# The low part of each split weight tile: an accumulating transfer in place of a GpSimd subtraction

## The chip, the core and the metric

The kernel runs on one core of a Trainium2 chip. The core has a matrix engine (TensorE, PE in the rows; its weight loads are PEld), VectorE (DVE), ScalarE (ACT), GpSimd (POOL), a queue engine that issues most transfers (SP), and 16 DMA engines that carry the transfers of all queues. The metric is the device time of one execution in microseconds, as a median over runs.

## The reference

Two layers of a diffusion backbone work on 128 context tokens and 512 latent tokens at once, with 1024 channels. Each layer has a mixing block and a SwiGLU FFN, and nearly all weight arithmetic is plain products of float32 arrays:

```python
proj = h @ p['w_in']
...
merged = (gates[:, :, 0] * (y_a @ p['w_pa']) + gates[:, :, 1] * (y_b @ p['w_pb'])
          + gates[:, :, 2] * (y_c @ p['w_pc']))
return merged.astype(h.dtype) @ p['w_o'], s_fin
...
gu = h @ w_gu
gate, up = jnp.split(gu, 2, axis=-1)
return (jax.nn.silu(gate) * up) @ w_down
```

Here `y_a` comes from a chunked gated DeltaNet, `y_b` from a long convolution and `y_c` from a Fourier mixer. Each sub-layer is preceded by an RMSNorm with shifts and scales that come from a conditioning vector through `w_mod`.

## The kernel before

**Split products.** Activations stand as channels on the 128 partitions by 640 tokens, which are worked on in two chunks of 320. TensorE multiplies in a rounded float32 form (`F32R`). So that the product is exact enough, each operand is cut into a high part, its rounding, and a low part, what the rounding left over; `mm3` then makes three matmuls for each 128 x 128 block of weights: high by high, high by low, low by high. `gemm` runs `mm3` over the blocks of a tile for one chunk of tokens.

**Weights.** Each weight is used once per execution. `wplan` lists raw tiles (128 x 1024, 512 KB, two buffers with the tag `wr`) in the order of use, and units of up to 512 columns that are split at once. `wload` issues raw loads on SP's queue. `wsplit` makes the two parts of a unit: ScalarE rounds it into `wh`, GpSimd subtracts the rounding from the raw values into `wl`. Each of the two tags has four buffers that turn; some units are parked in wide `A` tiles in their place. `free` is called when the last use of a unit has been issued, and splits further units up to four ahead of the one in use. `wget` and `wuse` hand the parts to the products.

**The FFN.** For all but two of a layer's 22 hidden tiles, gate and up are made by `pair`: seven products over blocks in place of eight. A pair has two raw tiles and seven units: three are quarters of the raw tiles, four are sums of quarters that VectorE makes in `U` tiles (`wsum`). Each product is 12 matmuls of 320 columns, in `prod`, which frees its unit at its end. After every three or four hidden tiles come eight output tiles of the down projection, whose units serve 18 or 24 matmuls.

**Order.** The instruction streams are written out by the program itself. A planner (`tick`) counts an estimated end for each instruction on five clocks (`pe`, `dve`, `act`, `pool`, `dma`). Side streams (the DeltaNet scans, filters, norms, and the conditioning columns that VectorE makes from `w_mod` loads) give steps that `pump` puts between the matmuls when their inputs are due by these clocks. Every engine runs its own stream in order, and waits on semaphores. The planner charges a GpSimd subtraction of 512 columns 0.1 + 512/450 us on `pool`; a `dma_start` from any engine is charged on `dma`, by bytes plus 2.0 us:

```python
if eng == "dma" or op == "dma_start":
    t = max(t, c["dma"], c["pe"] if cur is None else cur.t0) + n * out.shape[0] * 4 / 3.6e5
    c["dma"] = t
    t += 2.0
```

All instructions go through one helper, so nearly all rows name line 2185, and are told apart by tile names.

Of the kernel before, what the change touches and what calls it, by code (L numbers as in the profile page):

```python
# [71 lines left out]
def _plan():  # L72
    """the order of use: whole tiles, and pairs of a gate and an up tile for the seven products"""
    p = [("w", k) for k in _stream() if k[0] not in ("g", "u", "d")]
    for kind, g in _ffn_order():
        if kind == "gu":
            for j in GROUPS[g]:
                p += [("s", j)] if j >= WHOLE else [("w", ("g", j)), ("w", ("u", j))]
        else:
            p += [("w", ("d", g, m)) for m in range(0, 8, 2)]  # L80
    return p
# [9 lines left out]
def _parked(key):  # L91
    """whether the split tile stays for one half of the tokens after the other, in a place of its own"""
# [13 lines left out]
# ---------------------------------------------------------------- tables that depend on shapes alone  # L106
# [126 lines left out]
# ---------------------------------------------------------------- layout of the inputs  # L233
# [67 lines left out]
class _Net:  # L301
# [21 lines left out]
    # ---- allocation  # L323
# [19 lines left out]
    def xps(self):  # L343
        """a bank of either pool"""
        self.nps += 1
        return self.ps() if self.nps % 2 else self.gps()
# [8 lines left out]
    # ---- background work: each step of a side stream is issued once the tensor engine's work issued  # L355
    # so far reaches, by the engines' rates, the time when the step's inputs are there
    def when(self, *aps):
        """the time when what was issued has written these"""
# [36 lines left out]
    def on(self, *tiles):  # L395
        """the next step of the stream that runs needs these"""
        self.cur.t = max(self.cur.t, self.when(*[x[:] if not hasattr(x, "ap") else x for x in tiles]))

    def at(self, *tiles):
        """the next step of the stream that runs needs these and nothing of its other steps"""  # L400
# [7 lines left out]
    def ready(self, co):  # L408
        """a stream may yield a test (the time when it is met, or None) or a time its next step may
        be issued early"""  # L410
# [18 lines left out]
    def pump(self):  # L429
        """the streams' ready steps, as long as the main stream keeps its share of the tensor engine"""  # L430
# [19 lines left out]
    def finish_one(self, cos):  # L450
        """the next step of several streams, or of one that they wait for"""
# [6 lines left out]
    def stagger(self, gens, width):  # L458
        """several streams, `width` at a time, each behind the one before it"""
# [32 lines left out]
    # ---- weights  # L492
    def wplan(self, depth):
        """raw tiles in the order of their loads, and units: up to 512 columns that are split at once"""
# [24 lines left out]
    def wload(self, need=-1):  # L519
        """loads of raw tiles up to `need`, and further ones whose room is free by now"""  # L520
# [10 lines left out]
    def wsum(self, r, x):  # L531
        """sums of the four blocks of a gate and an up tile"""
# [12 lines left out]
    def wsplit(self, n):  # L545
        """units up to n, split in two float32r parts"""
        nc = self.nc
        while self.nunit <= n:
# [10 lines left out]
            else:  # L559
# [3 lines left out]
                lo = self.pw.tile([P, 512], F32R, tag="wl", name=self.nm("wl"), bufs=4)  # L563
            nc.scalar.copy(hi[:, :w], src)
            nc.gpsimd.tensor_tensor(out=lo[:, :w], in0=src, in1=hi[:, :w].bitcast(F32), op=ALU.subtract)
# [10 lines left out]
    def wget(self, key):  # L576
        """the units of the next item: all at once, or of a pair one after the other"""
# [13 lines left out]
    def lots(self, n):  # L591
        """places for the next n parked units"""
# [6 lines left out]
    def free(self, seen, drop):  # L599
        """so many more units have come to use, and so many of those in turning buffers had their last"""  # L600
# [32 lines left out]
    def rsqrt(self, r, m):  # L633
        """r = m ** -0.5, Newton's steps from a guess by the bits of m"""
# [9 lines left out]
    # ---- start  # L644
# [30 lines left out]
    def mods(self, l, lo, hi, par=False, ahead=1, hint=0.5):  # L675
        """adaLN columns lo..hi (of 48) of layer l, one per output channel tile"""
# [43 lines left out]
    def mods_pe(self):  # L720
        """the first 4 * MP adaLN columns of layer 0, on the tensor engine"""
# [45 lines left out]
    # ---- RMSNorm  # L767
    def sq_add(self, k, c=None):
        """running sum of the squares of x's channel tile k, on all tokens or a chunk of them"""
# [11 lines left out]
    def rstd(self, u, n, w):  # L781
        """1 / rms(x) of n * w tokens from u on, on all partitions"""
# [23 lines left out]
    def wait(self, c):  # L806
        """for 1 / rms(x) of a chunk"""
# [3 lines left out]
    def norm(self, l, gcol, sh, scl, new, place):  # L811
        """h = rmsnorm(x) * (1 + sc) + sh, split in two float32r parts"""
# [37 lines left out]
    def need(self, n):  # L850
        """steps of the norm until n channel tiles of chunks of h are issued"""
# [13 lines left out]
    def norm_blocks(self, l, gcol, sh, scl):  # L865
        """h by blocks (half of the channels) x (half of the tokens), and the sums of blocks for the seven
        products"""
# [34 lines left out]
    # ---- x in and out of DRAM  # L902
# [4 lines left out]
    # ---- Hyena's filters  # L907
    def sin_mlp(self, ps, M, scale, bias, out, n):
        """out = sin(scale * ps + bias), the argument brought within half a turn first"""
# [15 lines left out]
    def filters(self, l):  # L925
        """spectra of the two-sided filters of both orders, kept in DRAM"""
# [44 lines left out]
        def weights(z, o):  # L971
            """taps of h0 + h1 (real part) or h0 - h1 (imaginary part)"""
# [87 lines left out]
    # ---- input projection  # L1060
    def evict(self, dst, ps, c, func=AF.Copy, scale=1.0):
        """dst[:, 0:640] gets a chunk of 320 tokens"""
        self.nc.scalar.activation(dst[:, c * NC:(c + 1) * NC], ps[:, :NC], func, scale=scale)

    def conv_tile(self, wcol, l, raw=None, o=None):
        """room for a channel tile before and after the centred three-tap convolution: 128 prompt columns,
        one unused, 512 sample columns"""
# [21 lines left out]
    def proj_conv(self, key, wcol, l):  # L1089
        """one channel tile through w_in and the convolution"""  # L1090
# [6 lines left out]
    def permute(self, dst, src, fn, goff=1):  # L1097
        """token order of the delta tiles: tile s < 4 holds sample chunks s and 7 - s, tile 4 the prompt"""
# [6 lines left out]
    # ---- gated DeltaNet  # L1105
# [1130 lines left out]
```

## Time and profile before

| | us |
|---|---|
| median of 3 runs | 2922.06 |
| lowest and highest | 2921.55, 2927.12 |
| span of the profiled execution | 2920.5 |
| TensorE busy in it | 2570.7 (88%) |
| VectorE busy | 2191.0 (75%) |
| GpSimd busy | 1372.3 (47%) |
| ScalarE busy | 1017.4 (35%) |

The profiled execution has no time of its own besides its span, which is 1.6 us below the median of the runs. Matmuls overlap in the pipeline, and each is shown with its whole latency, so their pace is read from the starts of a group and not from the mean duration of one. A wait is named by what released it. Busy time of an engine leaves out the sequencer's work, the issuing of transfers among it.

### The profile page before, as it was taken

What the parts mean: (1) busy time and instruction counts of PE and PEld (TensorE: products, weight loads), DVE (VectorE), ACT (ScalarE), POOL (GpSimd) and SP (SyncE); (2) the same over time, 40 slices, a digit from 0 to 9 for tenths busy, and PEclk for the clock granted to TensorE, in tenths of its full rate; (3) what the DMA queues carried; (4) which work ended last, traced back from release to release, by engine and by line L of the source; (5) the groups of instructions that cost most, each with busy time, mean ns of one, the idle gap of its engine ahead of it and who ended that gap; (6) DMA issues with size and microseconds to landing.
All of it is one profiled execution on the core that took longest, in us unless ns stands there. A gap on an engine that the chain in (4) does not pass through costs nothing. (4 is left out here: it accounts for less than half of the span.)

```text
span 2920.5 us, 53508 instructions
## 1 busy us (share of the span) xinstructions
PE 2570.7 (88%) x20996; PEld 2423.8 (83%) x20996; DVE 2191.0 (75%) x4162; ACT 1017.4 (35%) x2148; POOL 1372.3 (47%) x1228
## 2 busy tenths in 40 slices
PE   5897879879998888888898988788899988999998
PEld 1686878879998888878897768788899988999997
DVE  7787996774647899889966679977746468877665
ACT  2454223322332243223334552333323322444342
POOL 2333425442335475555543436353523354777662
PEclk8898989989999899999998999899999998999999
DMA  7442221343554223333322221212335542222222
GB/s 277 143 151 84 71 83 54 103 144 130 201 185 152 86 90 114 105 118 105 109 96 93 94 88 68 83 53 97 134 130 199 187 152 73 66 80 88 79 80 80
DMA packets 112044, 330.35 MB, mean 113 GB/s; under 512 B 12186, under 2 KB 26522, under 8 KB 103776
## 3 DMA queue, kind: packets, MB, share of 16 engines
q1 hardware_dynamic: 110352, 319.06, 31.9%
q0 software_dynamic: 1440, 7.87, 0.8%
q8 instruction: 165, 2.70, 0.4%
q14 instruction: 87, 0.71, 0.1%
HBM read 294.89 MB, written 37.24 MB: 114 GB/s over the span
## 5 line engine op out<-in xcount | busy, mean ns | idle before, releaser
L2185 PE MATMUL pg<-A,wh 128*128 128x320 f32 (+1 forms) x6304 | 1491.7, 324 | 115.3 <-DVE T L2185 46.5
L2185 PEld LDWEIGHTS pg<-A,wh 128*128 128x128 f32 (+1 forms) x6304 | 1096.4, 196 | 168.7 <-issue 56.5
L2185 POOL TENSOR_TENSOR wl<-wr,wh 128x512 fp32r<-128x512 f32 (+2 forms) x486 | 694.5, 1444 | 813.0 <-ACT wh L2185 773.9
L2185 PE MATMUL pg<-A,wl 128*128 128x320 f32 (+1 forms) x3152 | 1005.9, 319 | 1.3 <-POOL wl L2185 1.1
L2185 PEld LDWEIGHTS pg<-A,wl 128*128 128x128 f32 (+1 forms) x3152 | 618.0, 196 | 4.6 <-POOL wl L2185 3.4
L2185 ACT CAST wh<-wr 128x512 fp32r<-128x512 f32 (+2 forms) x486 | 284.4, 611 | 399.6 <-PE pg L2185 287.6
L2185 PE MATMUL ps<-A,wh 128*128 128x320 f32 x1696 | 386.7, 315 | 15.4 <-ACT wh L2185 15.4
L2185 DVE CUSTOM_DVE_ANT_0 A<-U,A 128x512 f32<-128x512 f32 x336 | 324.8, 967 | 14.3 <-DMA U<-in_wmod_dram 7.0
L2185 PEld LDWEIGHTS ps<-A,wh 128*128 128x128 f32 x1696 | 292.1, 193 | 16.9 <-ACT wh L2185 16.7
L2185 PE MATMUL ps<-A,wl 128*128 128x320 f32 x848 | 268.4, 316 | 8.0 <-POOL wl L2185 7.7
L2185 PE MATMUL ps<-A,A 32*32 32x32 f32 (+5 forms) x2984 | 212.1, 248 | 51.1 <-DVE A L2185 49.3
L2185 POOL TENSOR_TENSOR wl<-U,wh 128x512 fp32r<-128x512 f32 x160 | 238.2, 1509 | 30.7 <-ACT wh L2185 30.6
L2185 PEld LDWEIGHTS ps<-A,A 32*32 32x32 f32 (+2 forms) x2984 | 183.7, 150 | 63.1 <-DVE A L2185 50.6
L2185 DVE TENSOR_TENSOR A<-A 128x120 f32<-128x120 f32 (+22 forms) x690 | 209.5, 367 | 11.7 <-DMA A<-hyS 8.8
L2185 POOL TENSOR_TENSOR A<-A,A 128x640 fp32r<-128x640 f32 (+5 forms) x84 | 121.0, 1453 | 161.0 <-ACT A L2185 153.0
L2185 PE MATMUL pg<-A,A 128*128 128x320 f32 x1056 | 168.2, 319 | 10.0 <-ACT A L2185 9.6
L2185 PEld LDWEIGHTS ps<-A,wl 128*128 128x128 f32 x848 | 163.6, 193 | 12.0 <-POOL wl L2185 11.9
L2185 PEld LDWEIGHTS pg<-A,A 128*128 128x128 f32 x1056 | 162.7, 195 | 12.7 <-ACT A L2185 9.8
L2185 DVE TENSOR_TENSOR T<-T,T 128x320 f32<-128x320 f32 (+1 forms) x139 | 120.8, 869 | 68.0 <-ACT T L2185 63.0
L2185 ACT CAST wh<-U 128x512 fp32r<-128x512 f32 x160 | 99.1, 621 | 168.5 <-PE pg L2185 51.3
L2185 DVE STREAM_TRANSPOSE A<-A 32x1024 f32<-32x1024 f32 x72 | 148.8, 2092 | 1.3
L2185 DVE TENSOR_TENSOR U<-ps,U 128x512 f32<-128x512 f32 x144 | 78.0, 543 | 92.0 <-PE ps L2185 64.8
(164 smaller groups left out, 3085.8 us busy)
## 6 DMA issues: line engine op xcount, KB each, us to landing
wr<-in_wbig_dram SPq DMA_DIRECT2D x272, 512.0 KB, 3.7
U<-in_wmod_dram SPq DMA_DIRECT2D x168, 256.0 KB, 4.3
A<-hT SPq DMA_DIRECT2D x32, 1024.0 KB, 8.7
kSp<-U SPq DMA_DIRECT2D x40, 256.0 KB, 2.0
U<-kSp SPq DMA_DIRECT2D x40, 256.0 KB, 5.5
hyS<-T SPq DMA_DIRECT2D x24, 320.5 KB, 3.3
A<-in_wm_dram SPq DMA_DIRECT2D x6, 1024.0 KB, 11.0
A<-in_cc_dram SPq DMA_DIRECT2D x6, 1024.0 KB, 5.3
```

What stands on the lines that cost most here:

```text
L2185: return f(*a, **k)
```

## The change

In `wsplit`, ScalarE writes the negated rounding of the unit into the low buffer (a copy with scale -1 into an `F32R` tile). A transfer on GpSimd's queue then adds the raw unit onto it, element by element, in the DMA engines. ScalarE's rounding copy into the high buffer comes after these two in program order. The GpSimd subtraction is gone.

```diff
                 hi = self.pw.tile([P, 512], F32R, tag="wh", name=self.nm("wh"), bufs=4)
                 lo = self.pw.tile([P, 512], F32R, tag="wl", name=self.nm("wl"), bufs=4)
+            nc.scalar.activation(lo[:, :w], src, AF.Copy, scale=-1.0)
+            nc.gpsimd.dma_start(lo[:, :w], src, accum_op=ALU.add)
             nc.scalar.copy(hi[:, :w], src)
-            nc.gpsimd.tensor_tensor(out=lo[:, :w], in0=src, in1=hi[:, :w].bitcast(F32), op=ALU.subtract)
             self.whl[self.nunit] = (hi, lo)
```

The rest of the diff takes out comments and docstrings. The splits of activations (`split`) still subtract on GpSimd or VectorE.

## Rows read from the trace of the kernel before

**Rows 1.** First part of the page: busy time of each engine.
```profile
PE 2570.7 (88%) x20996; PEld 2423.8 (83%) x20996; DVE 2191.0 (75%) x4162; ACT 1017.4 (35%) x2148; POOL 1372.3 (47%) x1228
```

**Rows 2.** Stretches of both FFNs: us; PE, PEld, DVE, ACT, POOL; clock; DMA; GB/s.
```profile
1035.00:1490.00 455.00, 395.14 (x2446) 385.04 (x2445) 411.95 (x701) 153.14 (x287) 265.71 (x178) 0.92 0.33 108
2500.00:2850.00 350.00, 347.23 (x2340) 344.46 (x2339) 259.22 (x374) 146.07 (x274) 247.08 (x173) 1.00 0.25 79
```

**Rows 3.** Waits of TensorE, first FFN: total, times, longest.
```profile
PE pg L2185 <- DVE T L2185: 35.6, 15, 5.2
PE ps L2185 <- ACT wh L2185: 15.4, 5, 4.0
PE ps L2185 <- POOL wl L2185: 5.4, 7, 2.1
```

**Rows 4.** Waits of TensorE, second FFN, 2500 to 2850 us.
```profile
PE ps L2185 <- POOL wl L2185: 2.3, 2, 2.1
```

**Rows 5.** Chain that ended last, one product of the second FFN.
```profile
2584.74 1.76 PE ps L2185 x12
```

**Rows 6.** The page's groups: GpSimd's subtractions; out<-in, count, busy, mean ns.
```profile
L2185 POOL TENSOR_TENSOR wl<-wr,wh 128x512 fp32r<-128x512 f32 (+2 forms) x486 | 694.5, 1444 | 813.0 <-ACT wh L2185 773.9
...
L2185 POOL TENSOR_TENSOR wl<-U,wh 128x512 fp32r<-128x512 f32 x160 | 238.2, 1509 | 30.7 <-ACT wh L2185 30.6
```

**Rows 7.** GpSimd's groups by shape: the subtractions into parked places.
```profile
L2185 POOL TENSOR_TENSOR A<-wr,A 128x512 fp32r<-128x512 f32 x52 | 72.9, 1420 | 54.8 <-ACT A L2185 54.7
```

**Rows 8.** ScalarE's groups by shape: the rounding copy.
```profile
L2185 ACT CAST wh<-wr 128x512 fp32r<-128x512 f32 x452 | 268.5, 619 | 376.2 <-PE pg L2185 274.1 <-DMA wr<-in_wbig_dram 55.1 <-issue 34.0
```

**Rows 9.** Timeline, first FFN: start us, us, engine, what.
```profile
1304.12 0.69 DVE L2185 CUSTOM_DVE_ANT_0 A<-U,A 128x512 f32<-128x512 f32 x1
...
1305.70 1.30 POOL L2185 TENSOR_TENSOR wl<-wr,wh 128x512 fp32r<-128x512 f32 x1 [2.17 <-ACT wh L2185]
...
1305.79 1.76 DVE L2185 CUSTOM_DVE_ANT_0 A<-U,A 128x512 f32<-128x512 f32 x1
```

**Rows 10.** VectorE's groups by shape, first FFN.
```profile
L2185 DVE CUSTOM_DVE_ANT_0 A<-U,A 128x512 f32<-128x512 f32 x136 | 133.9, 984 | 3.4 <-DMA U<-in_wmod_dram 1.1
L2185 DVE TENSOR_TENSOR T<-T,T 128x320 f32<-128x320 f32 x40 | 38.6, 965 | 14.8 <-ACT T L2185 12.3 <-DVE T L2185 0.5
L2185 DVE TENSOR_TENSOR U<-wr,U 128x512 f32<-128x512 f32 x19 | 29.4, 1547 | 0.0
L2185 DVE TENSOR_TENSOR T<-T,pg 128x320 f32<-128x320 f32 x62 | 28.9, 479 | 0.3
...
L2185 DVE TENSOR_TENSOR U<-wr,wr 128x512 f32<-128x512 f32 x19 | 24.6, 1297 | 0.0
```

**Rows 11.** DMA queue and issues: KB each, median us to landing.
```profile
q1 hardware_dynamic: 110352, 319.06, 31.9%
...
wr<-in_wbig_dram SPq DMA_DIRECT2D x272, 512.0 KB, 3.7
U<-in_wmod_dram SPq DMA_DIRECT2D x168, 256.0 KB, 4.3
```

**Rows 12.** A 256 KB transfer on GpSimd's queue: issue ns, landing us.
```profile
L2185 POOL DMA_DIRECT2D U<-in_cd_dram x2: 607/607/607, 634.1 to 2094.1; - x2
...
DMA to landing us min/median/max: 3.1/3.6/4.1
```

**Rows 13.** Timeline, one split in the first FFN.
```profile
1133.25 0.62 ACT L2185 CAST wh<-U 128x512 fp32r<-128x512 f32 x1 [1.14 <-PE ps L2185]
...
1133.95 1.29 POOL L2185 TENSOR_TENSOR wl<-U,wh 128x512 fp32r<-128x512 f32 x1 [0.47 <-ACT wh L2185]
```

**Rows 14.** Timeline, three splits together, second FFN.
```profile
2592.97 1.65 ACT L2185 CAST wh<-wr 128x512 fp32r<-128x512 f32 x3
...
2593.66 4.85 POOL L2185 TENSOR_TENSOR wl<-wr,wh 128x512 fp32r<-128x512 f32 x3 [3.46 <-ACT wh L2185]
```

**Rows 15.** Waits, whole span: TensorE for VectorE's A tiles.
```profile
PE ps L2185 <- DVE A L2185: 69.5, 33, 14.9
```

## The prediction

> **What bounds the kernel now.** I read the busy shares of the page first. TensorE is busy 88% of the span, VectorE 75%, GpSimd 47%, ScalarE 35% [rows 1]; TensorE sets the end, and what can be won is its idle time. Next I cut the span into stretches, because the FFNs use the split weights fastest. The two are alike in work and unlike in their limit [rows 2]. In the second, TensorE is busy 347.2 of 350 us; one product of 12 matmuls takes 1.76 us [rows 5], a pair of seven 12.3 us, and a single wait of note is left [rows 4]. In the first, TensorE is busy 395.1 of 455 us while VectorE is busy 412 us, since the conditioning columns of the next layer are made there too. The list of waits names VectorE's T tiles with 35.6 us and ScalarE's `wh` with 15.4 us [rows 3]. So the first FFN has 59.9 us of idle TensorE to give, the second next to none.
>
> The timeline then shows why VectorE is late. One of its column instructions takes 0.69 us when GpSimd rests, and the next one, started just after a subtraction of 1.30 us, takes 1.76 us: it ends 0.55 us after the subtraction does [rows 9]. The groups of the first FFN say the same: two tiles in SBUF added over 320 columns take 965 ns, an SBUF and a PSUM operand 479 ns [rows 10]. The subtraction that the change removes is what VectorE stands behind.
>
> **What is removed.** 698 subtractions (486 + 160 + 52) of 694.5 + 238.2 + 72.9 = 1006 us on GpSimd [rows 6, 7]. GpSimd is not on the path; its waits as a releaser in the first FFN are 5.4 us [rows 3]. The value lies in VectorE. In the first FFN the 136 column instructions lose 0.984 - 0.69 = 0.29 us each, 40 us; the 40 T additions lose 0.965 - 0.479, 19 us; the two kinds of sums, 19 each, fall from 1.547 and 1.297 us to about 0.69 (an estimate: the undisturbed instruction of the same 512 columns), 28 us [rows 9, 10]. That is 87 us of 412; VectorE is left with 325 us, under TensorE's 395, and stops being the bound. What TensorE may then win is its 35.6 us for T and 15.4 us for `wh`, whose casts wait for those sums: 51 us at most [rows 3]. Outside the FFNs TensorE waits 69.5 us for VectorE's A tiles [rows 15]. These are chains, and only their instructions with two SBUF operands shrink; I take a quarter, 17 us, between nothing and the whole.
>
> **What is added on ScalarE.** 698 copies of 0.62 us [rows 8] are 432 us on 1017, half of the span. They are hidden by its idle time. Where they are not, `wh` comes 0.62 us later, since the negated copy stands first: five waits for `wh` in the first FFN [rows 3] make 3 us, and evictions behind a copy that waits for its buffer as much again. I take 7 us, between none and about 20.
>
> **What is added on the queues.** GpSimd issues 698 transfers of 0.61 us [rows 12], 424 us of sequencer time for the 1006 us it loses; work queued behind them gets earlier. If the copy is late, GpSimd's stream stands at the transfer, with the low parts of activations behind it, as it stood for `wh` before. A raw tile is now read until the transfer has landed, so the next 512 KB load, which waits in SP's stream, starts later, with the `w_mod` loads behind it.
>
> **Latency.** A split shows its subtraction 0.70 us after ScalarE's start [rows 13] and lasts 1.3 us: 2.0 us. A 256 KB transfer on GpSimd's queue lands 3.1 to 4.1 us after its issue [rows 12]; an accumulating one must also read its destination. At the hardware queue's rate, 319.06 MB in 31.9% of 2920.5 us or 342 GB/s [rows 11], one more reading is 0.77 us. So the low part is there after 0.70 + 3.9 to 4.9 = 4.6 to 5.6 us. In a pair the unit is wanted when three other products are done, 5.3 us, and two matmuls more [rows 5], about 5.5 us. It just fits. Against it: three splits came out of ScalarE in one go, 4.85 us of subtractions [rows 14], because ScalarE had stood before a slower instruction; such a bunch has no slack. For it: a faster VectorE makes these bunches rarer. In stages with 24 matmuls a unit there is twice the time, and the latency is covered.
>
> **Rate.** No row shows an accumulating transfer. Its time on the 16 engines lies between 0.77 us (one pass) and, reading both operands at the same rate, 1.53 us; a slower adder would go beyond, and bounds nothing but the range. I take 1.3 us, nearer to two readings; the queue's rate mixes lengths and HBM, and both operands here are in SBUF. A pair then needs 7 x 1.3 + 2 x 1.53 (two raw loads) = 12.2 us of the engines against 12.3 us of TensorE: nearly full, no longer idle. Queueing costs something: I price it at half of the spread of landings, 0.5 us a pair, over 20 pairs 10 us in the second FFN. In the first the engines also carry 24 down tiles at 1.53 + 2 x 1.3 = 4.1 us and 68 `w_mod` loads (two column instructions each) at 0.77: 244 + 99 + 52 = 395 us, as much as TensorE's own. Two full resources seldom meet; I take half of the 51 us, 26.
>
> On this price the Trainium skill has a rule. Collectives: The Full Stack, section "The bandwidth ceiling", says that an add in the transfer path is not slow in itself, but reads two sources on one ring and so runs at half the rate of a copy. No row here shows it. By it the transfer is the 1.53 us above, the second FFN loses 20 x (13.8 - 12.3) = 30 us, the first wins 455 - 438 = 17 us, and the sum below would be +3 us.
>
> **Sum.** First FFN -26, second +10, elsewhere -17, ScalarE +7: -26 us. The span of 2920.5 us becomes 2894.5; the median stands 1.6 us above the span, so 2896 us. Bounds: with one pass the first FFN may give all 51 and the second lose nothing, with 17 elsewhere, near 2855. Where the engines are the bound in both FFNs, a transfer that holds them for x us makes the sum about 328x - 500 us: 188x - 305 in the first FFN (20 pairs of seven, 24 tiles of two, against 455 us), 140x - 185 in the second (against 20 x 12.3), -10 elsewhere. It changes sign at x = 1.5 us.
>
> **Rivals.**
> *The forecast*, x under 1.5 us: VectorE freed, the engines just keep up. 2896 us, by itself 2850 to 2918. Chance 0.48.
> *The adding transfer sets the pace*, slower than before. At x = 2.0 a pair takes 7 x 2.0 + 3.07 = 17.1 us; the sum is +156 us, 3078 us; at 3.0 it is some +480. It decides from 1.5 us on, just where two plain readings lie. For it: nothing here has shown such a transfer, and rows of 2 KB are half as long as the raw tiles'. Against it: DMA engines are a quarter busy in the second FFN [rows 2]. Chance 0.34.
> *Late low parts*: the rate holds, the latency does not. Of two transfers alike one landed 1.0 us later [rows 12]. Suppose that a low part takes 6.5 us where 5.5 us fit: four products lose 1.0 us, the 280 products 70 us, and the gains leave about +35: 2957 us. Chance 0.08. SBUF — State Buffer, section "Who interferes with whom", gives one cause: VectorE copies and scalar operations in a two-port mode keep GpSimd from writing descriptors, while additions of two tensors do not. The costly groups of the first FFN are additions and column products [rows 10], so little of this is to be expected; no run here shows it yet.
> *No difference*: what the first FFN wins, the second and ScalarE lose. It also covers that the planner, which now charges the split 0.73 + 2.0 us on its `dma` clock, puts side work elsewhere. 2922 us. Chance 0.10.
>
> **How the numbers follow.** 0.2% of the median is 6 us, about what a measurement can tell. Faster holds the forecast, 0.48; same 0.10; slower the other two, 0.42. Low end 2850, just beyond the one-pass bound. High end 3050, x = 1.9: it takes in late low parts and the nearer half of the slow adder, and leaves out some 0.16 above and 0.04 below.
>
> **What would show it.** Column instructions near 0.7 us and T additions near 0.48 us: the gain is there. VectorE under 340 us in the first FFN. TensorE's waits by name: if `wl` transfers stand on top in the pairs, read their landing time; 5 us or less is the forecast, over 6 the latency rival, and DMA engines full throughout the pairs the pace rival. Products of 1.76 us without gaps in the second FFN mean that it is all hidden. The prediction is wrong if an accumulating transfer holds the engines over 1.5 us, or if VectorE's faster instructions leave TensorE's waits where they were.

## The result, and the profile after

The changed kernel takes 2966.81 us (median of 4 runs, 2959.48 to 2984.03) against 2921.81 us (4 runs, 2919.41 to 2927.12) on the same chip. The ratio is 1.0153 [1.0118, 1.0188]: 1.5% slower. The forecast was 2896 us, and faster; the time lies inside the range and on its other side. The profiled execution has a span of 2957.7 us.

Busy times of the engines after the change, from the page, and the two DMA queues that matter (packets, MB, share of 16 engines):

```profile
PE 2581.8 (87%) x20996; PEld 2419.3 (82%) x20996; DVE 1839.0 (62%) x4162; ACT 1381.3 (47%) x2846; POOL 966.8 (33%) x1228
...
q0 software_dynamic: 101952, 188.54, 35.3%
q1 hardware_dynamic: 110352, 319.06, 32.8%
```

GpSimd's busy time, unlike what is said of busy times ahead, holds the issuing of its transfers: 602.5 of its 966.8 us (419.7 + 138.0 + 44.8 for low parts from raw tiles, from sums and in parked places).

VectorE has lost 352 us of 2191.0 [rows 1], as its instructions no longer stand behind a subtraction. Its groups in the first FFN (count | busy us, mean ns) show it; before they took 984 and 965 ns [rows 10]:

```profile
L2187 DVE CUSTOM_DVE_ANT_0 A<-U,A 128x512 f32<-128x512 f32 x128 | 88.1, 688 | 2.5
...
L2187 DVE TENSOR_TENSOR T<-T,T 128x320 f32<-128x320 f32 x40 | 19.7, 493 | 75.2 <-ACT T L2187 73.2
```

That much went as forecast, and yet the kernel is slower. The stretches of both FFNs, as in [rows 2], and two of 15 us inside groups of pairs of the second:

```profile
1035.00:1490.00 455.00, 385.85 (x2406) 374.28 (x2407) 274.93 (x672) 236.06 (x445) 148.18 (x172) 0.94 0.89 197
2500.00:2850.00 350.00, 309.94 (x2015) 301.56 (x2014) 154.43 (x319) 193.96 (x368) 122.20 (x144) 0.98 0.83 175
2590.00:2605.00 15.00, 13.23 (x88) 12.70 (x88) 7.04 (x15) 10.47 (x21) 5.97 (x8) 1.00 0.93 197
2605.00:2620.00 15.00, 13.67 (x93) 13.28 (x92) 6.27 (x14) 9.69 (x21) 6.83 (x8) 1.00 0.91 181
```

The DMA engines are at 0.83 to 0.93 where they were at 0.25 and 0.33. TensorE is busy 310 of 350 us in the second FFN, where it had been 347. The list of TensorE's waits over the whole span (us, times, longest) names what has become of it:

```profile
PE pg L2187 <- DMA wl<-U: 58.5, 35, 3.2
...
PE ps L2187 <- DMA wl<-U: 35.0, 29, 3.3
```

Nearly all of this lies in the pairs. First the first FFN (1020 to 1465 us), then the second (2469 to 2876 us):

```profile
PE pg L2187 <- DMA wl<-U: 37.1, 18, 3.2
PE ps L2187 <- DMA wl<-U: 16.0, 13, 3.3
```

```profile
PE pg L2187 <- DMA wl<-U: 20.8, 16, 3.2
PE ps L2187 <- DMA wl<-U: 15.1, 14, 2.6
```

In the first FFN the waits for T and `wh`, 35.6 + 15.4 us before [rows 3], are gone from the list, and 53.1 us for the low parts of the sums stand in their place. In the second these are 35.9 us, where 2.3 us of waits had been left [rows 4]. Others' waits show the second effect, those of ScalarE, VectorE and the queue that issues the raw loads:

```profile
ACT wl L2187 <- DMA wr<-in_wbig_dram: 169.7, 60, 6.4
...
DVE U L2187 <- DMA wr<-in_wbig_dram: 77.4, 20, 9.8
```

```profile
SPq L2187 <- DMA wl<-wr: 1686.0, 244, 37.6
```

The low parts of the sums (`wl<-U`) arrive late, and ScalarE and VectorE wait for raw tiles, which are held until a transfer has read them: the queue of the raw loads stood 941.0 us for GpSimd's subtractions before, and stands 1686.0 us for the transfers now. The DMA issues (KB, median us to landing) give the size:

```profile
wr<-in_wbig_dram SPq DMA_DIRECT2D x272, 512.0 KB, 4.2
wl<-wr POOLq DMA_DIRECT2D x452, 256.0 KB, 4.0
...
wl<-U POOLq DMA_DIRECT2D x160, 256.0 KB, 6.6
```

**Stages.** The casts `wh<-U` occur in pairs only, so their first and last starts mark where the pairs of each layer begin and end. Rows of the tile `wh`, first layer and second (duration ns, first and last start us):

```profile
L2187 ACT CAST wh<-U x80: 600/602/609, 1020.5 to 1464.2; 128x512 fp32r<-128x512 f32 x80
...
L2187 ACT CAST wh<-U x80: 600/602/618, 2468.8 to 2875.5; 128x512 fp32r<-128x512 f32 x80
```

The same rows of every run give this table (us; "end" is from the last such cast to the end, "sum" the span of the profiled execution, "run" the median of all runs, which lies up to 15 us from it, so that a few us in one stage of one execution tell little):

```
kernel                       to 1st  1st FFN  between  2nd FFN  end   sum     run
before                       1030.5  440.7    1016.1   352.7    80.5  2920.5  2921.8
after                        1020.5  443.7    1004.6   406.7    82.2  2957.7  2966.8
e1  no transfer               997.5  345.0     963.6   344.8    79.6  2730.5  2731.3
e2  before, with copy        1033.6  446.7    1027.7   362.9    81.1  2952.0  2955.3
e3  same order               1033.1  446.6    1018.5   408.6    84.1  2990.9  3001.0
e4  transfers outside pairs  1019.2  464.6    1013.8   367.1    81.1  2945.8  2946.9
e5  five T tiles             1020.1  425.6    1007.7   402.3    81.6  2937.3  2944.0
e6  low part one ahead       1076.3  440.0    1041.3   425.8    82.5  3065.9  3068.9
e7  plain transfer            988.3  388.9     981.6   365.7    78.6  2803.1  2809.4
e8  fewer raw loads          1025.6  407.2    1006.5   383.8    87.6  2910.7  2906.0
e9  three raw buffers        1016.4  419.5    1002.2   398.9    83.9  2920.9  2915.4
e10 room for e9              1019.1  430.1    1008.6   405.3    81.5  2944.6  2945.3
e11 transfers for sums       1038.2  424.4    1018.1   384.1    79.5  2944.3  2940.2
e12 GpSimd writes only        958.2  344.4     943.9   345.0    80.1  2671.6  2675.4
e13 before, three raw        1028.7  437.0    1013.4   352.6    80.6  2912.3  2914.5
e14 three raw, low ahead     1020.2  402.8     997.1   382.1    81.7  2883.9  2886.3
e15 VectorE subtracts        1050.6  398.2    1037.6   363.3    79.7  2929.4  2929.3
e16 VectorE for the sums     1019.4  401.5    1010.8   389.8    84.0  2905.5  2903.0
e17 e16, low ahead           1020.2  387.4     997.6   378.5    80.2  2863.9  2878.5
e18 mixed                    1018.1  390.4     994.3   358.9    80.2  2841.9  2853.4
```

So the change gives 10 us before the first FFN and 11.5 between the two, and loses 3 in the first, 54 in the second and 2 at the end: 37 us of span.

### The profile page after: what moved, and what is told of

The parts are those of the page before. It is cut to its first block, busy times and chain, and to the rows that moved or that the text cites. A ratio compares the mean times of both kernels' runs of the same rounds, so it can differ in the third digit from the quotient of the medians.

```text
span 2957.7 us, 54779 instructions
## 1 busy us (share of the span) xinstructions
PE 2581.8 (87%) x20996; PEld 2419.3 (82%) x20996; DVE 1839.0 (62%) x4162; ACT 1381.3 (47%) x2846; POOL 966.8 (33%) x1228
## 3 DMA queue, kind: packets, MB, share of 16 engines
q0 software_dynamic: 101952, 188.54, 35.3%
## 5 line engine op out<-in xcount | busy, mean ns | idle before, releaser
L2187 POOL DMA_DIRECT2D wl<-wr x486 | 419.7, 880 | 1112.2 <-ACT wl L2187 980.5
L2187 ACT ACTIVATE wl<-wr 128x512 fp32r<-128x512 f32 (+2 forms) x486 | 303.1, 624 | 482.0 <-PE pg L2187 270.6
L2187 ACT CAST wh<-wr 128x512 fp32r<-128x512 f32 (+2 forms) x486 | 290.6, 598 | 0.0
L2187 DVE CUSTOM_DVE_ANT_0 A<-U,A 128x512 f32<-128x512 f32 x336 | 247.7, 737 | 17.2 <-DMA U<-in_wmod_dram 9.7
L2187 DVE TENSOR_TENSOR T<-T,T 128x320 f32<-128x320 f32 (+1 forms) x139 | 72.4, 521 | 232.7 <-ACT T L2187 227.7
L2187 POOL DMA_DIRECT2D wl<-U x160 | 138.0, 867 | 161.7 <-ACT wl L2187 137.9
L2187 POOL TENSOR_TENSOR A<-A,A 128x640 fp32r<-128x640 f32 (+5 forms) x84 | 127.4, 1552 | 135.5 <-ACT A L2187 125.0
L2187 DVE TENSOR_TENSOR A<-A 128x120 f32<-128x120 f32 (+23 forms) x690 | 158.4, 296 | 13.8 <-DMA A<-hyS 10.7
```

What stands on the lines that cost most here:

```text
L2187: return f(*a, **k)
```

## The experiments

**Theory.** Removing GpSimd's reading gains far more than forecast; the transfer loses more than that, because the low parts of the sums come later than TensorE wants them and raw tiles are held longer. **Rivals:** the DMA engines are full in the pairs and set the pace; the adding itself is nearly free and ScalarE's second copy costs; the planner, which charges the split otherwise, has moved side work to worse places. Runs e1 to e18 are compared with the kernel before on the same chip; all ratios are to it.

**e1, the transfer left out.** The low part is the negated rounding alone.

```diff
             nc.scalar.activation(lo[:, :w], src, AF.Copy, scale=-1.0)
-            nc.gpsimd.dma_start(lo[:, :w], src, accum_op=ALU.add)
```

> The changed kernel without its accumulating transfers: the negated copy on ScalarE stays, the low part is left as the negated rounding (so the low part's value is wrong). Late-low-part theory and full-engines theory both: the stretch of the pairs falls from 444 to about 400 us in the first FFN and from 407 to about 353 us in the second, the rest stays some 20 us shorter than before; 2850 to 2870 us in all. ScalarE theory (the extra copies delay the splits): the pairs of the second FFN stay near 400 us and the whole above 2930 us.

Measured: 2731.26 us, 0.9341 [0.9316, 0.9366]. The stretches inside the two FFNs:

```profile
1000.00:1340.00 340.00, 340.00 (x2320) 339.99 (x2320) 276.06 (x677) 228.74 (x438) 3.82 (x2) 1.00 0.41 138
2310.00:2650.00 340.00, 340.00 (x2320) 340.00 (x2319) 182.87 (x370) 227.80 (x438) 3.82 (x2) 1.00 0.26 82
```

Both bands are missed, for the gain is about three times the one expected. TensorE never rests in these stretches, at a granted clock of 1.00, in the first FFN too, where it had 0.92 with its idle time [rows 2]. 190 us are to be had, and the transfer takes back 2966.8 - 2731.3 = 236 us.

**e2, the kernel before with the negated copy added;** GpSimd overwrites it by its subtraction.

```diff
+            nc.scalar.activation(lo[:, :w], src, AF.Copy, scale=-1.0)
             nc.scalar.copy(hi[:, :w], src)
             nc.gpsimd.tensor_tensor(out=lo[:, :w], in0=src, in1=hi[:, :w].bitcast(F32), op=ALU.subtract)
```

> The kernel before, with the negated copy added on ScalarE ahead of the rounding copy, and the GpSimd subtraction still making the low part. ScalarE theory: at least half of what the pairs of the second FFN lost, so 25 us or more there, and over 2945 us. Late-low-part and full-engines theories: under 10 us more than before, 2920 to 2932 us, since ScalarE is idle for over half of the span.

Measured: 2955.29 us, 1.0106 [1.008, 1.0132]. The copy costs 30 us beside the old subtraction, spread over all stages; the prediction had 7. The whole lies in the band of the ScalarE theory, but the second FFN loses 10 us and not its 25, so the copy has a price that the other theories left out and is not what the pairs lost. In this kernel the subtraction waits behind both copies, so 30 is its price there, and not surely in the changed one.

**e3, the changed kernel in the order that the planner had before:** copy and transfer are issued past its clocks, and a subtraction is charged in their place.

```diff
-            nc.scalar.activation(lo[:, :w], src, AF.Copy, scale=-1.0)
-            nc.gpsimd.dma_start(lo[:, :w], src, accum_op=ALU.add)
+            nc.scalar._e.activation(lo[:, :w], src, AF.Copy, scale=-1.0)
+            nc.gpsimd._e.dma_start(lo[:, :w], src, accum_op=ALU.add)
             nc.scalar.copy(hi[:, :w], src)
+            self.tick("pool", "tensor_tensor", lo[:, :w], [src, hi[:, :w]])
```

> The changed kernel with the planner charging each split what it charged before (a GpSimd subtraction), so that all engines get the order of instructions of the kernel before. Order theory (the planner puts side work in worse places): back to 2925 us or less. Late-low-part and full-engines theories: the pairs stay at about 440 and 405 us, the whole between 2950 and 2985 us.

Measured: 3000.99 us, 1.0245 [1.0182, 1.0309]. The second FFN stays at 408.6 us. In the trace VectorE's and TensorE's instructions stand in the order of the kernel before, by their tiles, and by the ratios the kernel is 27 us slower than in the planner's new order, above both bands. The planner is not the cause.

**e4, transfers only for units outside the pairs, and e11, only for the sums in them;** the others are subtracted by GpSimd. The negated copy and the transfer stand under the first condition, which in e11 is `x[0] == "s"`.

```diff
+            if x == "raw":
...
             nc.scalar.copy(hi[:, :w], src)
+            if not (x == "raw"):
+                nc.gpsimd.tensor_tensor(out=lo[:, :w], in0=src, in1=hi[:, :w].bitcast(F32), op=ALU.subtract)
```

> Transfers for all units but those of the pairs, which are subtracted on GpSimd as before. Late-low-part and full-engines theories: pairs as before, about 441 and 353 us; the gain of some 20 us outside stays; 2895 to 2910 us, faster than both kernels. If outside the pairs the change gains nothing by itself (its gain came from the pairs' order): 2920 us.

> Transfers only for the four sums of each pair, which VectorE makes in U tiles; everything that is read from a raw tile is subtracted on GpSimd as before, so no raw tile waits for a transfer. Raw-tile theory: raw loads start as before, four transfers and two raw loads need 8.2 of 12.3 us of the engines; the first FFN 400 to 425 us, the second 348 to 362 us, the whole 2880 to 2905 us, faster than both kernels. If collision with raw loads alone makes the transfers late, whoever holds the raw tiles: second FFN 375 us or more, the whole 2920 us or more.

Measured: e4 2946.86 us, 1.0073 [1.0047, 1.0098]; e11 2940.25 us, 1.0044 [1.0016, 1.0071]. Either mixture is slower than the kernel before. e4 misses both of its bands; its loss lies in the FFNs (464.6 and 367.1 us), whose pairs it leaves to GpSimd, and why is open. e11 lies in the band of the collision with raw loads (second FFN 375 us or more). In e11 the queue and the landing are telling:

```profile
q0 software_dynamic: 24480, 49.83, 8.7%
...
wl<-U POOLq DMA_DIRECT2D x160, 256.0 KB, 5.7
```

With a quarter of the changed kernel's load on this queue, the sums' low parts still take 5.7 us in the median, and the second FFN 384 us. That speaks for lateness and against pace, but GpSimd mixes both kinds of work here, and its order is a third cause that e11 leaves in.

**e5, the changed kernel with five T tiles for six,** a control for the room that later runs need.

```diff
-        self.pt = pool("pt", 6)
+        self.pt = pool("pt", 5)
```

> The changed kernel with five instead of six T tiles; it only makes room, and is what the next run is compared with. All theories: between 2955 and 3000 us, the pairs of the second FFN near 405 us.

Measured: 2944.0 us, 1.0069 [1.0044, 1.0095], 23 us under the change itself and below the band. A buffer less changes the time by some 20 us, for a reason that no run shows, so a difference of that size between two of these kernels proves no mechanism by itself. The runs that follow are compared with that of the nearest buffers.

**e6, copy and transfer one unit earlier** than the rounding copy, with five low buffers (and five T tiles). `wlow` makes these two, and `wsplit` keeps the rounding copy.

```diff
+        while self.nlow < min(self.nseen + 5, len(self.units)):
+            if not (self.lot if self.nlow in self.parked else self.nlout < 5):
+                break
+            self.wlow(self.nlow)
```

> The run with five T tiles, with five low buffers instead of four, and the negated copy and the transfer of a unit issued one product earlier (five ahead; the rounding copy stays four ahead). Late-low-part theory (transfers of the sums land after 5 to 6.6 us where 5.3 us fit, since they fly beside two raw loads): one product more is 1.76 us, nearly all waits for low parts go; pairs of the second FFN 355 to 375 us, the whole 50 us or more below the run with five T tiles. Full-engines theory (seven transfers and two raw loads fill the 16 DMA engines): an earlier issue brings no capacity; 395 to 410 us there, the whole within 15 us of the run with five T tiles.

Measured: 3068.9 us, 1.0495 [1.047, 1.0521], 125 us above e5, where one theory had 50 us less than e5 and the other within 15 us of it. Of the 125, 90 us lie before the first FFN and between the two. The waits have changed places: TensorE waits less for the low parts of the sums (38.3 us in all, after 93.5), but those for raw tiles have grown from 169.7 and 77.4 us:

```profile
ACT wl L2202 <- DMA wr<-in_wbig_dram: 299.1, 89, 9.1
DVE U L2202 <- DMA wr<-in_wbig_dram: 240.6, 35, 11.5
...
PE ps L2202 <- DMA wl<-U: 25.0, 30, 2.7
```

So with two raw buffers there is little to start earlier from: each raw tile is held until its transfers have landed, and the next load waits for that.

**e7, a plain transfer:** the low part is a copy of the raw unit, with nothing added.

```diff
-            nc.gpsimd.dma_start(lo[:, :w], src, accum_op=ALU.add)
+            nc.gpsimd.dma_start(lo[:, :w], src)
```

> The changed kernel with a plain transfer of the raw unit over the low buffer in place of the adding one (so the low part's value is wrong): same issue, same bytes written, one reading instead of two. If the adding itself is the cost (178 ns a row on an engine against 84 ns for a plain one), landings fall to 2.5 to 4 us, a pair needs 7.2 us of the engines, both FFN stretches come near 345 to 360 us and the whole to 2750 to 2820 us. If any transfer on this path is too late, the pairs of the second FFN stay above 385 us and the whole above 2900 us.

Measured: 2809.4 us, 0.9611 [0.9576, 0.9646].

```profile
q0 software_dynamic: 101952, 188.54, 21.3%
...
wl<-wr POOLq DMA_DIRECT2D x452, 256.0 KB, 2.5
...
wl<-U POOLq DMA_DIRECT2D x160, 256.0 KB, 4.3
```

The whole lies in the band of the adding as the cost; the first FFN, 388.9 us, does not reach its 345 to 360. Of the transfer's 236 us, 78 are there without the add, and 157 come with it. The same bytes hold the engines for 35.3% of 2957.7 us with the add and 21.3% of 2803.1 without: divided by 188.54 MB, 1.45 and 0.83 us for 256 KB. The landings are 1.5 and 2.3 us later with it, and GpSimd takes 0.86 us to issue one in the median, where a plain one takes 0.53; the 157 us hold this too.

**e8, fewer raw loads:** within a group, pairs after the first use its raw tiles again, so their weights are others'. 60 of the 272 raw loads of 512 KB are left out, 30 in each FFN.

```diff
+            if n in self.again:
+                self.wt[n] = self.wt[n - 2]
+            else:
...
```

> The changed kernel, in which pairs after the first of a group use the first one's raw tiles again, so 28 of 40 raw loads in the pairs of each FFN are left out (and the products are of wrong weights). Late-low-part theory, by collision with the raw loads: these pairs run at 12.3 to 12.8 us instead of 14.5 to 16; second FFN 355 to 370 us, the whole 2850 to 2890 us. If the transfers collide with each other alone (one every 1.76 us, each 1.4 us of the engines): pairs stay above 14 us and the whole above 2930 us.

Measured: 2905.98 us, 0.9931 [0.9909, 0.9953].

```profile
wl<-wr POOLq DMA_DIRECT2D x452, 256.0 KB, 4.0
wr<-in_wbig_dram SPq DMA_DIRECT2D x212, 512.0 KB, 4.1
...
wl<-U POOLq DMA_DIRECT2D x160, 256.0 KB, 3.8
```

Without two raw loads of 512 KB in their way the sums' transfers land after 3.8 us, not 6.6. The collision with the next pair's raw tiles is what made them the latest. ScalarE still waits 157.3 us for raw tiles (169.7 in the changed kernel), so it is not these that have changed. TensorE's waits for the sums fall from 53.1 to 15.9 us in the first FFN and from 35.9 to 9.9 in the second, and these stages by 36.5 and 22.9 us. But that is not all of the loss: the second FFN keeps 383.8 us, above the 355 to 370 of its theory, and the whole is above its 2890. TensorE now waits 15.4 us there for the low parts of the quarters, after 3.5.

**e9, three raw buffers, and e10, its control** with the same five T and seven U tiles and two raw buffers; **e13, the kernel before with e9's buffers.**

```diff
-            r = self.pw.tile([P, 1024], F32, tag="wr", name=self.nm("wr"), bufs=2)
+            r = self.pw.tile([P, 1024], F32, tag="wr", name=self.nm("wr"), bufs=3)
-            if n > need and n > 1 and self.spent.get(n - 2, math.inf) > self.clk["pe"]:
+            if n > need and n > 2 and self.spent.get(n - 3, math.inf) > self.clk["pe"]:
```

> The changed kernel with three raw buffers instead of two (five T tiles and seven U tiles make the room, as in the next run). Raw-tile theory (a raw tile is held until its transfers have landed, so the next raw load starts late, and then flies beside the transfers of the sums): ScalarE's and VectorE's waits for raw loads fall to a third, the second FFN from about 402 to 370 to 388 us, the groups with down tiles from 36 to 45 us back to 33 to 41; the whole 30 us or more below the next run. If only the low parts are late: these waits go too, but TensorE's 86 us for transfers stay, and the whole is within 15 us of the next run.

> The changed kernel with five T tiles and seven U tiles; only what the run before is compared with. All theories: 2935 to 2985 us.

> The kernel before with three raw buffers, five T tiles and seven U tiles, as the earlier kernel with the change and three raw buffers had them (ratio 0.9961). If the third raw buffer only repairs what the change broke, because a raw tile is now held until a transfer has landed, the kernel before gains nothing from it: TensorE is not short of raw tiles there, and five T tiles may cost a little, ratio 1.000 to 1.006. If the third raw buffer is worth 30 us to either kernel, it is 0.990, and the change itself is still a loss.

Measured: e9 2915.41 us, 0.9961 [0.9947, 0.9975]; e10 2945.32 us, 1.0065 [1.0044, 1.0086]; e13 2914.54 us, 0.9958 [0.9942, 0.9973]. ScalarE's wait for raw tiles, first in e9, then in e10:

```profile
ACT wl L2187 <- DMA wr<-in_wbig_dram: 18.1, 8, 6.4
```

```profile
ACT wl L2187 <- DMA wr<-in_wbig_dram: 179.5, 58, 6.4
```

The wait is nearly gone, and with it 30 us, so raw tiles held until the landing were a part of the loss; the second FFN, 398.9 us, stays above the 370 to 388 of that theory. The kernel before was expected to gain nothing from e9's buffers or as much as 30 us; it gains 0.4%, 12 us, and no run says which buffer brings them. So up to 12 of the 30 us may be worth as much to either kernel. With the same buffers the two kernels take the same time: that e9 is 0.4% under the kernel before is no merit of the change.

**e12, GpSimd only writes:** two fills of the low buffer (528 ns each) stand in place of each subtraction of the kernel before; the low part is zero.

```diff
-            nc.gpsimd.tensor_tensor(out=lo[:, :w], in0=src, in1=hi[:, :w].bitcast(F32), op=ALU.subtract)
+            for _ in range(2):
+                nc.gpsimd._e.memset(lo[:, :w].bitcast(F32), 0.0)
+            self.tick("pool", "tensor_tensor", lo[:, :w], [src, hi[:, :w]])
```

> The kernel before with two GpSimd fills of the low buffer in place of the subtraction (so the low part is zero): GpSimd is about as busy, but reads nothing in SBUF. Reading theory (VectorE instructions with two SBUF operands stand while GpSimd reads): VectorE's column instructions fall to 0.7 us, the first FFN from 441 to about 345 to 355 us, the whole to 2690 to 2740 us. If GpSimd's time and the order behind it are what costs: above 2880 us.

Measured: 2675.43 us, 0.9142 [0.9124, 0.9161]. The page's busy times, and a group of VectorE's inside the first FFN:

```profile
PE 2492.6 (93%) x20996; PEld 2367.5 (89%) x20996; DVE 1816.8 (68%) x4162; ACT 1023.5 (38%) x2148; POOL 1089.0 (41%) x1926
```

```profile
L2187 DVE CUSTOM_DVE_ANT_0 A<-U,A 128x512 f32<-128x512 f32 x126 | 86.7, 688 | 6.7 <-DMA U<-in_wmod_dram 4.6
```

The time is below the band of the reading theory (2690 to 2740 us), and far from the other. GpSimd is busy 1089 us, 722 of them with these fills, and VectorE's column instruction takes 688 ns, as in the changed kernel: it is not the occupied GpSimd that VectorE stands behind but its reading. A fill does not wait for the rounding copy, as the subtraction does, so some of the 246 us may be that wait.

**e15, VectorE subtracts,** in the kernel before.

```diff
-            nc.gpsimd.tensor_tensor(out=lo[:, :w], in0=src, in1=hi[:, :w].bitcast(F32), op=ALU.subtract)
+            nc.vector.tensor_tensor(out=lo[:, :w], in0=src, in1=hi[:, :w].bitcast(F32), op=ALU.subtract)
```

> The kernel before with each low part subtracted by VectorE in place of GpSimd: no transfer, no reading by GpSimd in the splits. VectorE gets 698 subtractions of about 0.6 us, 420 us, on the 1817 to 1839 us that it needs where GpSimd does not read for the splits: about 2250 us, evenly spread under 2700. If what the kernel before loses is GpSimd's reading beside VectorE's, the whole falls to 2700 to 2800 us. If VectorE in order becomes the bound in the first FFN (325 + 150 us of 455), that stage gains little, and the whole is 2850 to 2900.

Measured: 2929.27 us, 1.0015 [1.0003, 1.0027]; both bands missed. VectorE's groups over the whole span:

```profile
L2185 DVE TENSOR_TENSOR wl<-wr,wh 128x512 fp32r<-128x512 f32 x452 | 330.0, 747 | 211.6 <-ACT wh L2185 210.5 <-issue 0.3
...
L2185 DVE TENSOR_TENSOR wl<-U,wh 128x512 fp32r<-128x512 f32 x160 | 103.3, 686 | 19.2 <-ACT wh L2185 18.9 <-issue 0.2
```

VectorE does one in half of GpSimd's 1444 ns [rows 6], but its subtractions, 433 us here and 35 more into parked places, outweigh what it was slowed by: it is busy 2237.6 us, where it was 2191.0 [rows 1]. It also stands 210 us in order behind ScalarE. The first FFN gains 42 us; the stage before it and the one between lose 20 each, the second FFN 11.

**e14, three raw buffers and the low part one unit earlier; e16, three raw buffers and VectorE for the sums' low parts, transfers for all others; e17, e16 with the transfers one unit earlier.** e14 and e17 have six U tiles for e9's and e16's seven. Only the engine of the sums is new in the code:

```diff
+            if x[0] != "s":
...
             nc.scalar.copy(hi[:, :w], src)
+            if not (x[0] != "s"):
+                nc.vector.tensor_tensor(out=lo[:, :w], in0=src, in1=hi[:, :w].bitcast(F32), op=ALU.subtract)
```

> The change with three raw buffers and each negated copy and transfer made one unit earlier (five low buffers, five T tiles, six U tiles). Alone, the earlier transfer moved the wait to the raw tiles (3069 us), and the third raw buffer alone gave 2915. Theory of latency: with both, neither the low parts nor the raw tiles are late, and it falls to the region of the plain transfer, 2810 to 2850 us. Theory of full DMA engines: the pairs are paced by the engines whatever is started earlier, 14 to 15 us a pair, and it stays between 2890 and 2920.

> The change with three raw buffers, but the low parts of the four sums of a pair subtracted by VectorE, and transfers only for the quarters and the other units. A pair then has three transfers and two raw loads on the engines, 3 x 1.4 + 3.1 = 7.3 us of 12.3, and none of the low parts that landed late. Theory of latency and full engines together: the pairs go at 12.3 us, and the whole is 2720 to 2800 us. If it stays near 2900, something else than the sums' transfers sets the pace of the pairs.

> As the run before with three raw buffers and the sums' low parts on VectorE (2903 us, its pairs 401 and 390 us), but the three transfers that a pair still has are made one unit earlier, as in the run that had that for all seven (2886 us). In the second FFN that run had the DMA engines at a share of 0.60 only, and still TensorE waited for the low parts of the quarters. Theory of latency: with the transfers earlier that wait goes, the second FFN's pairs fall from 390 to 345 to 360 us and the whole to 2820 to 2860 us. Theory of full engines: a share of 0.60 was enough to pace it, nothing falls, 2890 to 2910.

Measured: e14 2886.26 us, 0.9868 [0.9847, 0.989]; e16 2903.02 us, 0.9918 [0.9901, 0.9934]; e17 2878.52 us, 0.9845 [0.9817, 0.9873]. e14 and e17 lie between the bands of their two theories. e16 is near 2900, the second case of its expectation: something else than the sums' transfers sets the pace of its pairs. The stages tell more. The second FFN's pairs, of e14 (2420 to 2802 us), e16 (2432 to 2821) and e17 (2405 to 2784):

```profile
2420.00:2802.00 382.00, 356.85 (x2354) 347.99 (x2353) 191.26 (x374) 233.41 (x441) 149.17 (x173) 0.99 0.89 187
```

```profile
2432.00:2821.00 389.00, 357.41 (x2335) 353.04 (x2335) 239.43 (x454) 189.69 (x362) 80.33 (x91) 0.97 0.58 131
```

```profile
2405.00:2784.00 379.00, 357.80 (x2357) 351.75 (x2356) 237.35 (x452) 188.84 (x363) 80.25 (x92) 0.98 0.58 133
```

With equal lead, the engines' share falls from 0.89 to 0.58 from e14 to e17, and the pairs from 382 to 379 us only: the load alone does not set their pace. Nor were the engines full in the changed kernel, for e14 makes the same transfers in these pairs in 382 us that took 407 there. With equal load, one unit more of lead brings 17 us in each FFN from e9 to e14, and 14 and 11 from e16 to e17. In one stage this is no more than what a buffer did in e5 (18 us in the first FFN), but TensorE's waits go with them: for the sums' low parts from 31.7 us (e9) to 21.3 (e14) in the second FFN, for the quarters' from 29.7 (e16) to 20.2 (e17). That speaks for lateness. But to free the sums from it was not enough: what TensorE then waits for, here in e17's second FFN, are the quarters' low parts:

```profile
PE ps L2211 <- DMA wl<-wr: 10.6, 6, 1.9
PE pg L2211 <- DMA wl<-wr: 9.6, 5, 2.4
```

The trace of e17 shows why. One of these eleven waits, on ScalarE, GpSimd and TensorE:

```profile
2438.19 0.47 ACT L2211 ACTIVATE T<-T 128x320 f32<-128x320 f32 x1 [0.96 <-DVE T L2211]
...
2439.08 0.63 ACT L2211 ACTIVATE wl<-wr 128x512 fp32r<-128x512 f32 x1
```

```profile
2440.00 0.85 POOL L2211 DMA_DIRECT2D wl<-wr  x1 [5.66 <-DVE T L2211]
```

```profile
2443.33 0.41 PE L2211 MATMUL pg<-A,wl 128*128 128x320 f32 x1 [1.78 <-DMA wl<-wr]
```

ScalarE, in order, stands before an instruction on T that waits for VectorE, and then makes the negated copies of two quarters in a bunch; GpSimd has stood 5.66 us before it issues. Each of the eleven waits is preceded by such a bunch behind T. So e17 is short of e1's 345 us by 34, of which 20 are these waits; a clock of 0.98 over 358 busy us would be some 7 more (an estimate). Two units of lead were not tried.

**e18, what did best in each stage:** as e17, but the second FFN's units are subtracted by GpSimd as before ("p"; "v" is VectorE, "t" the transfer).

```diff
+        if l == 1 and j >= _stream().index(("g", 0)):
+            return "p"
+        return "v" if x[0] == "s" else "t"
```

> The same, but every unit of the second FFN subtracted by GpSimd as in the kernel before. From the stages measured so far: start and between as with the transfers (1020 and 1000 us), first FFN with VectorE's sums and early transfers 385 to 400, second FFN 353 as before, end 78: 2836 to 2851 us, the fastest that computes the weights' low parts in full. If GpSimd's return loses the start of the second FFN or the earlier order does not fit it, 2870 to 2900.

Measured: 2853.43 us, 0.9759 [0.9737, 0.9782]; 2 us above the first band; the profiled span, 2841.9 us, is inside the sum of the stages. It beats the kernel before by 2.4%, and by the ratios the changed one by 3.9%.

## Why the prediction was wrong, point by point

**What bounds the kernel** was right: TensorE sets the end, the first FFN has idle time to give and the second none [rows 2].

**VectorE behind the subtraction** was right in mechanism and size: 688 and 493 ns against about 0.69 and 0.48 us forecast. e12 adds that it is the reading. The Trainium skill, SBUF — State Buffer, section "Who interferes with whom", says that a VectorE instruction with two SBUF inputs contends with a GpSimd instruction that reads SBUF, not with one that only writes it. Here 984 ns beside reads [rows 10] and e12's 688 ns beside writes agree.

**What TensorE may win from it** was mis-sized: 26 and 17 us, at most 51 and 69.5, where e1 gains 96 us in the first FFN and 33 + 53 us in the stages before and between. The waits that it named did go. But the working took them as the bound, and TensorE's 395 us as what the first FFN costs in any case. With the idle time the lower clock went too, and the same pairs took 345 us at 1.00.

**ScalarE**, 7 us: mis-sized; e2 gives 30, in the kernel before.

**The rate**, x = 1.3 us: measured 1.45, below the sign change at 1.5. By the forecast's own formula for full engines, 328 x 1.45 - 500 = -24 us, so the pace-setting transfer would not have made the kernel slower, and e14 beside e17 shows that the load alone did not. The rule of Collectives: The Full Stack in the Trainium skill, section "The bandwidth ceiling", by which an add costs two source reads (told there for a ReduceScatter), comes near: 1.45 us is 1.75 times the plain 0.83.

**Latency** is the step that failed: "It just fits." The budget had 0.70 us to the issue and 3.9 to 4.9 to the landing, against 5.5. For the quarters this held, with 4.0, as long as the sums were later still. For the sums it did not. The timelines of ScalarE, GpSimd and SP in the second FFN show them in a pair:

```profile
2592.95 0.63 ACT L2187 ACTIVATE wl<-U 128x512 fp32r<-128x512 f32 x1 [0.62 <-PE ps L2187]
```

```profile
2592.12 0.85 POOL L2187 DMA_DIRECT2D wl<-U  x1 [0.91 <-ACT wl L2187]
2593.88 0.85 POOL L2187 DMA_DIRECT2D wl<-U  x1 [0.91 <-ACT wl L2187]
```

```profile
2591.93 2.12 SPq L2187 DMA_DIRECT2D wr<-in_wbig_dram  x2
```

From the copy's start at 2592.95 to the issue at 2593.88 are 0.93 us, and 6.6 to the landing in the median make 7.5. The transfers of the sums start just as the next pair's two raw loads do, and e8 shows that it is these. The landing had been read from two transfers [rows 12] that flew at a DMA share of 0.25 and 0.47 (5 us of the kernel before from 634 and from 2093 us), where the pairs now have 0.84, and the issue takes 0.85 us where those took 0.61. So the queueing price of 0.5 us a pair was 54 / 20 = 2.7 us in the second FFN, of which 35.9 / 20 = 1.8 are TensorE's waits for the sums' low parts. The rival of the late low parts, given 0.08, was what came, and 6.6 us to the landing is over the 6 us that were to be its sign. Its cause by VectorE does not show: the sums' transfers are issued in 0.86 us in the median, 0.85 at the least. Its 2957 us beside the measured 2967 are luck: they were made of 36 us won and 70 lost, where 190 (e1) and 236 were measured. Neither of the two signs by which the prediction was to be wrong came, a transfer over 1.5 us or waits of TensorE that stay: it was wrong by its budget all the same.

**The bunches** out of ScalarE, named against the budget and not priced, are what holds the quarters in e17.

**The raw tile** read until the transfer has landed was named and not priced: it is up to 30 us (e9 against e10), of which 12 may be worth as much without the change (e13).

**The account** by runs: without GpSimd's reading and its wait -246 us (e12), e1 against e12 +56, none of it in the FFNs, which holds ScalarE's copy but was not taken apart (e2 says 30 beside the old subtraction), a transfer +78 (e7 against e1), its add +157 (after against e7): +45 us, which is the difference by construction. For the FFNs the last two are lateness in the main, by TensorE's waits and e8, and held raw tiles beside it (e9); that the same holds for the 23 and 41 us by which the stages before and between exceed e1's is only argued.

## What to carry to other kernels

Where work moves from an engine to a transfer, sum the time from the source to the landed result as it is when the other loads of the same stage start, not as the transfer lands alone, and compare it with the lead that the buffers give; a transfer that also reads a staging buffer holds it longer, and may need one buffer more there. What an engine costs its neighbour is found by taking its reading away, and each stage may want another engine: here the best kernel uses three ways to make the same low part.

## What the runs showed of the hardware that was not expected

- GpSimd's fills, 722 us of writing in place of the subtractions (e12), left VectorE's two-operand instruction at 688 ns; the subtractions, 1006 us of reading and writing, had made it 984.
- An adding transfer of 256 KB within SBUF holds the engines for 1.45 us, a plain one for 0.83; from raw tiles it lands after 4.0 instead of 2.5 us, and GpSimd issues it in 0.86 instead of 0.53 us.
- In the first FFN the granted clock was 0.92 with 60 us of idle time in 455 [rows 2] and 1.00 in e1 without any, so that to remove idle time gave more than the idle time: 96 us.
